# Attention maxima with a fused mask, the planner's durations changed, and more buffers in a hybrid trunk on one core

## The chip, the cores and the metric

One core of a Trainium2 chip runs the whole kernel: TensorE (PE) with its weight loads (PEld), VectorE (DVE), ScalarE (ACT), GpSimd (POOL), and 16 DMA engines whose transfers are all issued from SyncE's queue (SP). The metric is device time in microseconds. The kernel before took 2701.05 us, the median of 3 runs (2700.61 to 2704.6).

## The reference

One layer (D = 1024, 2048 rows, fp32): `h = RMSNorm(x)`, one wide projection of `h`, three branches, a gated merge, an output projection, a residual and a last RMSNorm. The change lies in the first branch, attention with a forget gate over 8 heads of 64, and in the merge.

```python
def block(args):                       # 128 queries against all keys
    s = jnp.einsum('bqhd,bkhd->bhqk', q_blk, k) * scale
    s = s + F_blk[..., :, None] - F[:, :, None, :]      # F: running sum of log-sigmoid
    s = jnp.where(pos[None, None, None, :] <= p_blk[None, None, :, None], s, -jnp.inf)
    p = jax.nn.softmax(s, axis=-1)
    return jnp.einsum('bhqk,bkhd->bqhd', p.astype(v.dtype), v)
...
proj = jnp.einsum('bsnc,ncd->bsnd', ys, w_branch)       # three branches
gate = jax.nn.sigmoid(gates + b_merge).reshape(B, S, N_BRANCH, D)
merged = jnp.sum(gate * proj, axis=2)
return x + merged @ w_out
```

The maximum that softmax subtracts cancels, so any number near it does, if all terms of a query use the same one.

## The kernel before

**Two streams of work.** PE is fed from two sources. A generator `dense()` goes through the wide projection (tiles `pd_in`), then the merge (tiles `pbr`, `pba`) and the output projection (`pout`). Every dense product is three fp32r matmuls, high times high, high times low, low times high. Beside it the parts of `part_side()` run one after the other: norm, logits, memory attention, the delta-rule branch (`part_gdn_a`, `part_gdn_inv`, `part_gdn_b`), then the attention (`part_fox`). A dense matmul is the filler wherever a part has to wait.

**What sets the order.** `Plan` counts planned time while the program is written out: `pl.act(n)`, `pl.dve(n)` and `pl.pool(n)` add a duration for n elements a partition to an engine and return when the result is there. A part yields a time from which it can go on; `run` takes the first part in its list that is ready at PE's planned time, and the dense generator if none is. So the planner's durations decide how many dense matmuls stand between a part's steps on PE. Dependencies and semaphores come from the tile framework, which may move an instruction ahead of others. The engines wait in hardware wherever the plan was too optimistic.

**The attention** (`part_fox`) works in 32 units n = (head h, group G of 512 queries, G = 0 to 3), each with three steps. `maxima()`: for every block of 512 keys and 128 queries, one matmul into `psm`, a mask on the diagonal block (L1108, an addition of `mneg`), a maximum along the keys (L1110) into `nmx`; then the maximum over blocks (L1116), split into a rounded high part and a rest (L1118, L1119) in columns 96 to 103 of `mt`, transposed by PE (`ptm`) and spread into rows 96 to 103 of `QA` (L1124), from which the next product subtracts it. `values()`: for every 128 keys, two matmuls into `pst` (L1227, L1228), two exponentials on ACT (L1234 rounded into `ph`, L1236), the rounding rest on DVE (`plo`, L1191), the running sum of `ph` on POOL (`acc`, L1214), two matmuls onto the values (L1253, L1254). `sums()`: the row sums through PE (`pL`), a trip through DRAM to `lr`, their total and its reciprocal (L1162, L1163), and the product with `oT` on POOL. PSUM has four banks that `psm` (at most two of them) and `pst` (at most three) share.

**The merge** runs as tiles of 128 by 512: `branch(n, g, ...)` goes over d = 0 to 7 for branch n and group g, in the order n = 1, 2, 0. A tile is 12 matmuls; DVE multiplies by the gate tile `gt` (L1463), POOL adds the earlier partial sum `pp` (n = 2 and 0 only, L1467), and the result is stored to `dpt`. `gt`, `pp` and the store are 256 KB each. All loads and stores stand in SP's one queue in program order, and a store waits there for POOL. Branch 0 of groups 0 and 1 needs the attention's results; groups 2 and 3 of it come last, as `pba`, when the attention's buffers are gone.

## Time and profile before

| | us |
|---|---|
| median of 3 runs | 2701.05 |
| the profiled execution | 2707.26 |
| its span, first to last instruction | 2705.4 |
| PE busy | 2593.4 |
| PE idle | 112.0 |
| DVE busy | 1434.6 |
| ACT busy | 1086.6 |
| POOL busy | 941.3 |

A row of the page is read so: "busy" is the time in which at least one instruction of the engine ran; "idle before" is the engine's idle time just ahead of a group, with the engine and line that ended it. [...] The attention runs from about 1511 us to about 2425 us.

### The profile page before, as it was taken

The page shows a single profiled execution, that of the slowest core. Times are in us where ns is not written, and L with a number is a line of the kernel's source. Part 1 is how long each engine was busy: PE and PEld are TensorE (multiplying, and loading weights), DVE is VectorE, ACT ScalarE, POOL GpSimd, SP SyncE. Part 2 cuts the span into 40 slices and gives each one's busy share as a digit, 9 for nine tenths or more (in the row PEclk, how much of TensorE's full clock was granted, in tenths as well). Part 3 has the DMA queues.
Part 4 walks back from the last instruction along what each step waited for, and adds up shares of the span by engine and source line. Part 5 has one row for each costly group of instructions (what it writes and reads, how often), then busy time and mean ns, then how long its engine had stood idle before and what let it go on. Part 6 is the DMA issues. An engine that isn't in the chain of part 4 may idle for free. (4 is left out here: it accounts for less than half of the span.)

```text
span 2705.4 us, 36503 instructions
## 1 busy us (share of the span) xinstructions
PE 2593.4 (96%) x12584; PEld 2119.3 (78%) x12584; DVE 1434.6 (53%) x2867; ACT 1086.6 (40%) x2269; POOL 941.3 (35%) x752
## 2 busy tenths in 40 slices
PE   7999999999999989999999999999999999988998
PEld 6778888888888867888878877877776777757887
DVE  6452556666435583122220287666767778764543
ACT  5442324442665311234332255545655445451221
POOL 0101110011344311122212266756766477783200
PEclk9999999999999999999999999999998999999999
DMA  5223231222667533455542343323326777638433
GB/s 197 70 80 117 75 98 63 71 78 76 204 234 238 195 123 131 120 166 150 160 147 90 117 128 118 102 93 108 96 71 202 229 211 223 207 99 254 169 125 109
DMA packets 264905, 375.00 MB, mean 139 GB/s; under 512 B 62464, under 2 KB 140416, under 8 KB 264464
## 3 DMA queue, kind: packets, MB, share of 16 engines
q1 hardware_dynamic: 264720, 372.68, 43.1%
q8 instruction: 99, 1.62, 0.3%
q14 instruction: 86, 0.70, 0.1%
HBM read 230.66 MB, written 141.92 MB: 138 GB/s over the span
## 5 line engine op out<-in xcount | busy, mean ns | idle before, releaser
L395 PE MATMUL pd_in<-hh,wh_in 128*128 128x512 f32 x1984 | 800.4, 403 | 19.3 <-DVE evl L425 14.4
L397 PE MATMUL pd_in<-hh,wl_in 128*128 128x512 f32 x1984 | 779.1, 393 | 1.0
L396 PE MATMUL pd_in<-hl,wh_in 128*128 128x512 f32 x1984 | 777.7, 392 | 0.0
L379 POOL TENSOR_TENSOR wl_in<-wr_in,wh_in 128x1024 fp32r<-128x1024 f32 x88 | 213.8, 2429 | 967.4 <-ACT wh_in L375 950.9
L395 PEld LDWEIGHTS pd_in<-hh,wh_in 128*128 128x128 f32 x1984 | 374.2, 189 | 102.1 <-DVE evl L425 19.4
L397 PEld LDWEIGHTS pd_in<-hh,wl_in 128*128 128x128 f32 x1984 | 373.9, 188 | 84.4 <-POOL wl_in L379 4.5
L396 PEld LDWEIGHTS pd_in<-hl,wh_in 128*128 128x128 f32 x1984 | 374.7, 189 | 68.9
L1214 POOL TENSOR_TENSOR acc<-acc,ph 128x512 f32<-128x512 f32 (+3 forms) x288 | 323.3, 1123 | 69.8 <-ACT ph L1234 50.4
L1234 ACT ACTIVATE ph<-pst 128x512 fp32r<-128x512 f32 (+1 forms) x320 | 170.6, 533 | 155.8 <-PE pst L1228 64.9
L1191 DVE TENSOR_TENSOR plo<-pst,ph 128x512 fp32r<-128x512 f32 (+1 forms) x320 | 192.0, 605 | 69.0 <-ACT pst L1236 66.8
L1110 DVE TENSOR_REDUCE nmx<-psm 128x1 f32<-128x512 f32 (+2 forms) x320 | 190.0, 605 | 39.9 <-PE psm L1105 37.1
L1236 ACT ACTIVATE pst<-pst 128x512 f32<-128x512 f32 (+1 forms) x320 | 170.9, 534 | 0.0
L375 ACT CAST wh_in<-wr_in 128x1024 fp32r<-128x1024 f32 x88 | 92.4, 1049 | 160.6 <-PE pd_in L396 142.1
L1438 PE MATMUL pbr<-yh,wbh 128*128 128x512 f32 x320 | 131.2, 412 | 7.0 <-DVE gt L1463 6.0
L1439 PE MATMUL pbr<-yl,wbh 128*128 128x512 f32 x320 | 129.3, 405 | 0.7 <-DVE yl L604 0.7
L1440 PE MATMUL pbr<-yh,wbl 128*128 128x512 f32 x320 | 128.9, 403 | 0.0
L1254 PE MATMUL pq<-plo,Vs 128*128 128x512 f32 (+1 forms) x320 | 118.7, 374 | 8.9 <-DVE plo L1191 8.9
L1227 PE MATMUL pst<-QA,KA 128*128 128x512 f32 (+1 forms) x320 | 118.2, 370 | 5.0 <-DVE nmx L1110 1.8
L1467 POOL TENSOR_TENSOR gt<-gt,pp 128x512 f32<-128x512 f32 x64 | 85.6, 1342 | 104.2 <-DVE gt L1463 93.5
L1253 PE MATMUL po<-ph,Vs 128*128 128x512 f32 (+1 forms) x320 | 119.4, 376 | 1.4 <-ACT ph L1234 1.2
L1105 PE MATMUL psm<-KA,QA 68*128 68x512 f32 (+2 forms) x320 | 114.8, 374 | 5.6 <-DVE nmx L1110 5.6
L466 DVE SCALAR_TENSOR_TENSOR evv<-xb,cw,evv 128x512 f32<-128x512 f32 x144 | 116.6, 809 | 3.7
(334 smaller groups left out, 4366.5 us busy)
## 6 DMA issues: line engine op xcount, KB each, us to landing
wr_in<-in_w_in SPq DMA_DIRECT2D x88, 512.0 KB
dgt<-evg SPq DMA_DIRECT2D x96, 256.0 KB
gt<-dgt SPq DMA_DIRECT2D x96, 256.0 KB
dpt<-gt SPq DMA_DIRECT2D x80, 256.0 KB
pp<-dpt SPq DMA_DIRECT2D x64, 256.0 KB
dgq<-evv SPq DMA_DIRECT2D x48, 256.0 KB
kqv<-dgq SPq DMA_DIRECT2D x16, 768.0 KB
xt<-in_x SPq DMA_DIRECT2D x16, 512.0 KB
```

Of the source, the lines that this page charges most:

```text
L379: nc.gpsimd.tensor_sub(lo, raw, hi.bitcast(F32))
L395: nc.tensor.matmul(ps, wh[:, k, :], xh[:, k, :], start=(k == 0), stop=False)
L396: nc.tensor.matmul(ps, wh[:, k, :], xl[:, k, :], start=False, stop=False)
L397: nc.tensor.matmul(ps, wl[:, k, :], xh[:, k, :], start=False, stop=(k == kt - 1))
L1110: nc.vector.tensor_reduce(nmx[:, j, ck:ck + 1], ps[:, 0:w], AX.X, ALU.max)
L1191: nc.vector.tensor_sub(plo[:, 0:w], ps[:, 0:w], ph[:, 0:w].bitcast(F32))
L1214: nc.gpsimd.tensor_add(acc[:, c0:512], acc[:, c0:512], ph[:, 0:w].bitcast(F32))
L1234: nc.scalar.activation(ph[:, 0:w], ps[:, 0:w], AF.Exp, scale=0.125)
L1236: nc.scalar.activation(ps[:, 0:w], ps[:, 0:w], AF.Exp, scale=0.125)
L1438: nc.tensor.matmul(ps, wh[:, k, :], yh, start=(k == 0), stop=False)
L1439: nc.tensor.matmul(ps, wh[:, k, :], yl, start=False, stop=False)
L1440: nc.tensor.matmul(ps, wl[:, k, :], yh, start=False, stop=(k == 3))
```

## The change

- **Mask and maximum.** The diagonal block's mask addition and the maximum become one `tensor_tensor_reduce` (add, then maximum); `mneg` grows to 512 columns. In the built program this is two instructions, the main one and one that writes the maximum out.
- **One rounded maximum a query.** The maximum over blocks is written straight into `mt` as one fp32r number, columns 96 to 99; the copy and the subtraction go, and rows 100 to 103 of `KA`, `QA` and `blk` with them.
- **Sums.** The total of the two halves in `lr` is a `tensor_reduce` over one input instead of an addition of two.
- **Planner.** Other durations for ACT, DVE, POOL, for the delta rule's inverse and for the step to `mt`. `sums` parts are put first in the list of parts.
- **Buffers.** `NQ` 3 to 4 (query tiles), three `psm` banks instead of two, `acc` 2 to 3, `OB` 3 to 4 (output tiles); `values()` may start when the sums of unit n - 3 are done, not n - 2.
- **Gate tiles.** In `branch` the gate tile is loaded two tiles ahead, the partial sum one tile ahead as before.

```diff
     def act(self, n, after=0.0):
-        return self.op("act", 0.2 + 0.00083 * n, after)
+        return self.op("act", 0.17 + 0.00085 * n, after)
     def dve(self, n, after=0.0):
-        return self.op("dve", 0.08 + 0.00104 * n, after)
+        return self.op("dve", 0.15 + 0.00105 * n, after)
     def pool(self, n, after=0.0):
-        return self.op("pool", 0.1 + 0.0022 * n, after)
+        return self.op("pool", 0.19 + 0.0022 * n, after)
...
-    def add(self, gen):
+    def add(self, gen, first=False):
...
-        self.parts.append(part)
+        self.parts.insert(0 if first else len(self.parts), part)
...
-                    t1 = pl.op("dve", 0.18 + 0.0021 * i * i, t1)
+                    t1 = pl.op("dve", 0.35 + 0.0027 * i * i, t1)
...
-        rs, rp = banks.user(2), banks.user(3)
+        rs, rp = banks.user(3), banks.user(3)
...
-        NK, NQ = 6, 3
+        NK, NQ = 6, 4
...
+                        mx = nmx[:, j, ck:ck + 1]
                         if ck == G:
-                            nc.vector.tensor_tensor(ps[:, w - P:w], ps[:, w - P:w], mneg, ALU.add)
-                            e = pl.dve(P, e)
-                        nc.vector.tensor_reduce(nmx[:, j, ck:ck + 1], ps[:, 0:w], AX.X, ALU.max)
+                            nc.vector.tensor_tensor_reduce(ps[:, 0:w], ps[:, 0:w], mneg[:, 512 - w:512], 1.0, -3e38,
+                                                           ALU.add, ALU.max, mx)
+                        else:
+                            nc.vector.tensor_reduce(mx, ps[:, 0:w], AX.X, ALU.max)
...
-                mx = nmx[:, :, 0]
-                if G:
-                    mx = fx.tile([P, 4], F32, tag="mx", name="mx", bufs=2)
-                    nc.vector.tensor_reduce(mx, nmx[:, :, 0:G + 1], AX.X, ALU.max)
-                mv = mt[:, 96:104].rearrange("p (j s) -> p j s", s=2)
-                nc.vector.tensor_copy(mv[:, :, 0], mx)
-                nc.vector.tensor_sub(mv[:, :, 1], mx, mv[:, :, 0].bitcast(F32))
-                t1 = pl.op("dve", 0.5, e)
+                nc.vector.tensor_reduce(mt[:, 96:100], nmx[:, :, 0:G + 1], AX.X, ALU.max)
+                t1 = pl.op("dve", 0.25, e)
...
-            nc.vector.tensor_tensor(rl, lr[:, 0], lr[:, 1], ALU.add)
+            nc.vector.tensor_reduce(rl, lr.rearrange("p s j -> p j s"), AX.X, ALU.add)
...
-                yield (lambda: mready.get(n, INF) if min(st["L"], st["gate"]) >= n - 1 else INF), 0.0
-                acc = fx.tile([P, 512], F32, tag="acc", name="acc", bufs=2)
+                yield (lambda: mready.get(n, INF) if st["L"] >= n - 2 and st["gate"] >= n - 1 else INF), 0.0
+                acc = fx.tile([P, 512], F32, tag="acc", name="acc", bufs=3)
...
-                pl.add(sums(n, oS, acc, fill["ta"]))
-
-        OB = 3
+                pl.add(sums(n, oS, acc, fill["ta"]), True)
+
+        OB = 4
...
-                if d < 7:
-                    load_gate(n, g, d + 1, True)
-                elif then:
-                    load_gate(*then, 0, True)
+                for e in (d + 1, d + 2):
+                    if e < 8:
+                        load_gate(n, g, e, e - d)
+                    elif then:
+                        load_gate(*then, e - 8, e - d)
...
-                pp = None
-                if n != 1:
-                    pp = bp.tile([P, 512], F32, tag="pp", name="pp", bufs=3)
-                    move(pp, dpt[n // 2][g][:, d, :], 256)
-                gates[n, g, d] = gt, pp
+                gates[n, g, d] = [gt, None]
+            ld = gates[n, g, d]
+            if n != 1 and ahead < 2 and ld[1] is None:
+                ld[1] = bp.tile([P, 512], F32, tag="pp", name="pp", bufs=3)
+                move(ld[1], dpt[n // 2][g][:, d, :], 256)
```

The planner's numbers move instructions on all engines. Three places follow, before and after, as the built programs have them.

DVE at the end of the last unit's maxima, before: the last diagonal block, then the step from `nmx` to `mt`.

```order
L1108 TENSOR_TENSOR psm<-psm,mneg 128x128
L1110 TENSOR_REDUCE nmx<-psm 128x1
L1116 TENSOR_REDUCE mx<-nmx 128x4
L1191 TENSOR_TENSOR plo<-pst,ph 128x512
L1118 CAST mt_12279<-mx 128x4
L1119 TENSOR_TENSOR mt_12279<-mx,mt_12279 128x4
```

The same place after (ISA is the fused instruction and its write-out; L1462 is the gate product, L1078 and L1121 are L1077 and L1124 of before).

```order
L1110 ISA psm,nmx<-psm,mneg 128x512
L1110 ISA nmx 128x1
L1116 TENSOR_REDUCE mt_12283<-nmx 128x4
L1078 TENSOR_TENSOR Vs_12230<-ptv,Vs_12230 128x4x64
L1462 SCALAR_TENSOR_TENSOR gt<-gt,pbr_1_20800 128x512
L1121 TENSOR_TENSOR QA_12223<-ptm,blk 4x512
```

From the last block's maximum to the transposed `mt` there is one instruction of DVE where there were three, with a fourth of another step among them.

PE near the end of the last unit's values, before:

```order
L1227 MATMUL pst<-QA_12221,KA_12209 128x512
L1228 MATMUL pst<-QB_12224,KB_12215 128x512
L1253 MATMUL po<-ph,Vs_12227 128x512
L1254 MATMUL pq<-plo,Vs_12227 128x512
L1227 MATMUL pst<-QA_12221,KA_12209 128x384
L1228 MATMUL pst<-QB_12224,KB_12215 128x384
```

The same key tiles after (L1224, L1225, L1250, L1251 are L1227, L1228, L1253, L1254 of before; L1436 to L1438 are a branch tile's matmuls, and `pbr_1` is branch 2, group 1, since the listing drops the branch's digit).

```order
L1224 MATMUL pst<-QA_12223,KA_12209 128x512
L1225 MATMUL pst<-QB_12227,KB_12215 128x512
L1250 MATMUL po<-ph,Vs_12229 128x512
L1251 MATMUL pq<-plo,Vs_12229 128x512
L1436 MATMUL pbr_1_21071<-yh,wbh_20419 128x512
L1437 MATMUL pbr_1_21071<-yl,wbh_20419 128x512
L1438 MATMUL pbr_1_21071<-yh,wbl_20421 128x512
L1224 MATMUL pst<-QA_12223,KA_12209 128x384
L1225 MATMUL pst<-QB_12227,KB_12215 128x384
```

Before, the last unit's steps follow each other with nothing between them; after, matmuls of branch 2 stand between them. Behind the last `pL` of the attention there are 10.5 branch tiles before and 26.75 after, all ahead of the first `pba`.

SP's queue where branch 2 ends and branch 0 begins, before (`dpt_3` is the store of branch 2, group 3; `dgt_115` and `dpt_0` are the gate and the partial sum for branch 0, group 0; `wbr` a weight tile of branch 0):

```order
L243 DMA dpt_3_134<-gt 128x512
L243 DMA wbr<-in_w_br 128x512 x2
L243 DMA lr<-dL_227 128x2x4
L243 DMA dya_121<-oT 64x512
L243 DMA za<-dza_101 64x512
L243 DMA gt<-dgt_115 128x512
L243 DMA pp<-dpt_0_131 128x512
```

The same place after:

```order
L243 DMA dpt_3_134<-gt 128x512
L243 DMA pp<-dpt_3_138 128x512
L243 DMA wbr<-in_w_br 128x512
L243 DMA gt<-dgt_115 128x512
L243 DMA dpt_3_134<-gt 128x512
L243 DMA pp<-dpt_0_131 128x512
```

The attention's small transfers are gone from here, and the next branch's gate tile is asked for before branch 2's stores are all out.

## Rows read from the trace of the kernel before

**Rows 1.** The page's first part: busy time of an engine over the whole span, its share, instructions.
```profile
PE 2593.4 (96%) x12584; PEld 2119.3 (78%) x12584; DVE 1434.6 (53%) x2867; ACT 1086.6 (40%) x2269; POOL 941.3 (35%) x752
```

**Rows 2.** The busy time of each engine in nine stretches: the stretch (us), its length, then PE, PEld, DVE, ACT and POOL busy with their instructions, the granted clock of TensorE as a share of 2.4 GHz, the mean busy share of the 16 DMA engines, GB/s.
```profile
0.00:430.00 430.00, 400.49 (x1935) 329.13 (x1936) 221.61 (x385) 162.07 (x261) 50.77 (x29) 0.98 0.32 103
430.00:900.00 470.00, 464.49 (x2248) 381.83 (x2247) 250.97 (x563) 228.31 (x603) 123.64 (x105) 1.00 0.45 147
900.00:1100.00 200.00, 185.55 (x825) 149.66 (x824) 109.58 (x175) 36.10 (x71) 36.48 (x25) 0.99 0.39 134
1100.00:1511.00 411.00, 406.60 (x2375) 342.17 (x2374) 83.77 (x190) 144.42 (x303) 87.68 (x52) 1.00 0.45 140
1511.00:1800.00 289.00, 287.43 (x1328) 231.72 (x1327) 187.19 (x404) 140.78 (x273) 171.10 (x148) 1.00 0.38 117
1800.00:2350.00 550.00, 524.97 (x2349) 421.21 (x2348) 401.29 (x792) 268.28 (x540) 361.02 (x306) 0.98 0.53 162
2350.00:2427.00 77.00, 65.13 (x256) 45.32 (x255) 57.64 (x111) 46.56 (x95) 67.82 (x58) 0.96 0.35 107
2427.00:2473.00 46.00, 36.77 (x157) 29.23 (x155) 13.56 (x20) 4.09 (x7) 18.38 (x15) 0.92 0.81 249
2473.00:2705.00 232.00, 221.95 (x1125) 189.03 (x1125) 109.02 (x229) 56.01 (x118) 24.42 (x17) 0.98 0.45 151
```

**Rows 3.** What PE waited for between 1800 and 2350 us: total us, times, longest.
```profile
PE ptm L1123 <- DVE mt L1119: 8.1, 6, 2.8
PE psm L1105 <- DVE nmx L1110: 5.1, 6, 2.8
PE ptv L1075 <- DVE nmx L1110: 3.9, 2, 2.7
PE pq L1254 <- DVE plo L1191: 3.2, 1, 3.2
```

**Rows 4.** The timeline of DVE, of POOL and of PE near 1838 us: start, duration, engine, line, operation; in brackets the idle time before it and what ended it.
```profile
1835.31 3.65 DVE L1118 CAST mt<-nmx 128x4 fp32r<-128x4 f32 x1
1838.88 0.15 DVE L1162 TENSOR_TENSOR rl<-lr 128x4 f32<-128x4 f32 x1
...
1836.61 2.33 POOL L379 TENSOR_TENSOR wl_in<-wr_in,wh_in 128x1024 fp32r<-128x1024 f32 x1
...
1839.22 0.32 PE L1123 MATMUL ptm<-ident,mt 128*104 128x128 f32 x1 [2.83 <-DVE mt L1119]
```

**Rows 5.** DVE's groups by shape between 1511 and 2427 us: line, operation, out<-in, count | busy us, mean ns of one | idle before.
```profile
L1191 DVE TENSOR_TENSOR plo<-pst,ph 128x512 fp32r<-128x512 f32 x224 | 152.9, 685 | 56.0 <-ACT pst L1236 54.3
L1110 DVE TENSOR_REDUCE nmx<-psm 128x1 f32<-128x512 f32 x224 | 151.3, 686 | 38.6 <-PE psm L1105 37.1
...
L1108 DVE TENSOR_TENSOR psm<-psm,mneg 128x128 f32<-128x128 f32 x128 | 36.1, 293 | 26.8 <-PE psm L1105 25.6
...
L1162 DVE TENSOR_TENSOR rl<-lr 128x4 f32<-128x4 f32 x31 | 21.7, 701 | 14.7 <-DMA lr<-dL 14.7
...
L1118 DVE CAST mt<-mx 128x4 fp32r<-128x4 f32 x24 | 13.9, 577 | 0.5
...
L1119 DVE TENSOR_TENSOR mt<-mx,mt 128x4 fp32r<-128x4 f32 x24 | 10.3, 429 | 0.5
...
L1118 DVE CAST mt<-nmx 128x4 fp32r<-128x4 f32 x8 | 8.9, 1112 | 0.0
...
L1119 DVE TENSOR_TENSOR mt<-nmx,mt 128x4 fp32r<-128x4 f32 x8 | 4.5, 558 | 0.1
...
L1116 DVE TENSOR_REDUCE mx<-nmx 128x4 f32<-128x16 f32 x8 | 1.3, 167 | 0.2
```

**Rows 6.** The one DVE line that also writes out a running sum: min/median/max ns of the main instruction and of the reading of the accumulator.
```profile
L329 DVE SCALAR_TENSOR_TENSOR jkv<-xt x2: 1204/1638/2073, 5.8 to 12.1; 128x1024 f32<-128x1024 f32 x2
L329 DVE DVE_READ_ACCUMULATOR jkv<-xt x2: 77/79/81, 6.9 to 14.1; 128x1 f32 x2
```

**Rows 7.** Two more groups by shape, of POOL (all of the span) and of ACT (1500 to 2410 us), columns as in the group of DVE.
```profile
L1214 POOL TENSOR_TENSOR acc<-acc,ph 128x512 f32<-128x512 f32 x192 | 250.7, 1306 | 44.1 <-ACT ph L1234 34.7
...
L1234 ACT ACTIVATE ph<-pst 128x512 fp32r<-128x512 f32 x223 | 133.1, 597 | 93.2 <-PE pst L1228 64.9 <-DVE pst L1231 9.7 <-issue 7.2
```

**Rows 8.** PE's timeline: its longest wait behind 1511 us.
```profile
2398.47 0.79 PE L1254 MATMUL pq<-plo,Vs 128*128 128x512 f32 x1 [4.88 <-DVE plo L1191]
```

**Rows 9.** The branch tiles behind the attention: the first matmul, the last eviction and the first matmul of the next stage in the timelines of PE and DVE, and what PE waited for between 2427 and 2480 us.
```profile
2427.57 0.39 PE L1438 MATMUL pbr<-yh,wbh 128*128 128x512 f32 x1
...
2466.42 0.69 DVE L1463 SCALAR_TENSOR_TENSOR gt<-gt,pbr 128x512 f32<-128x512 f32 x1 [2.89 <-PE pbr L1440]
...
2473.13 1.01 PE L1563 MATMUL pba<-yh,wbh 128*128 128x256 f32 x3 [3.57 <-ACT yh L603]
...
PE pbr L1438 <- DVE gt L1463: 5.8, 3, 3.3
```

**Rows 10.** What the DMA queue of SP waited for between 2427 and 2473 us.
```profile
SPq L243 <- POOL gt L1467: 18.0, 9, 3.9
```

**Rows 11.** One stretch in which PE does almost nothing but 512-column matmuls, columns as in the nine stretches.
```profile
600.00:700.00 100.00, 100.00 (x449) 82.96 (x448) 59.31 (x96) 32.49 (x63) 12.66 (x6) 1.00 0.31 92
```

**Rows 12.** What PE waited for between 900 and 1100 us.
```profile
PE pd_in L395 <- DVE evl L425: 14.4, 10, 4.5
```

More of the change, by code (lines that the diff above doesn't have):

```diff
@@ L1021, in part_fox @@
         ones = fx.tile([P, P], F32R, name="ones")
-        mneg = fx.tile([P, P], F32, name="mneg")
+        mneg = fx.tile([P, 512], F32, name="mneg")
         nc.gpsimd.memset(mneg, 0.0)
-        nc.gpsimd.affine_select(mneg, mneg, [[-1, P]], ALU.is_ge, -1e30, base=0, channel_multiplier=1)
+        nc.gpsimd.affine_select(mneg[:, 384:512], mneg[:, 384:512], [[-1, P]], ALU.is_ge, -1e30, base=0,
+                                channel_multiplier=1)
         mnegT = fx.tile([P, P], F32, name="mnegT")
@@ L1033, in part_fox @@
             nc.vector.memset(KA[i][64:68].bitcast(F32), 1.0)
-            nc.vector.memset(KA[i][96:104].bitcast(F32), -1.0)
+            nc.vector.memset(KA[i][96:100].bitcast(F32), -1.0)
             nc.gpsimd.memset(Vs[i][:, :, P:192].bitcast(F32), 2.0)
@@ L1038, in part_fox @@
         nc.gpsimd.memset(blk, 1.0)
-        nc.gpsimd.affine_select(blk, blk, [[-2, 4], [0, P]], ALU.is_ge, 0.0, base=-96, channel_multiplier=1)
-        nc.gpsimd.affine_select(blk, blk, [[2, 4], [0, P]], ALU.is_ge, 0.0, base=97, channel_multiplier=-1)
-        mts = [fx.tile([P, 104], F32R, name=f"mt{i}") for i in range(2)]
+        nc.gpsimd.affine_select(blk, blk, [[-1, 4], [0, P]], ALU.is_ge, 0.0, base=-96, channel_multiplier=1)
+        nc.gpsimd.affine_select(blk, blk, [[1, 4], [0, P]], ALU.is_ge, 0.0, base=96, channel_multiplier=-1)
+        mts = [fx.tile([P, 100], F32R, name=f"mt{i}") for i in range(2)]
         for i in range(2):
@@ L1447, in dense, with load_gate @@
         gates = {}
-        def load_gate(n, g, d, ahead=False):
+        def load_gate(n, g, d, ahead=0):
             if (n, g, d) not in gates:
```

6 lines of the change are left out of this document (3 added, 3 removed).

## The prediction

> **What bounds the kernel now.** I read the busy times first: PE is busy 2593.4 of 2705.4 us, so 112.0 us of idle time are all that a better order can win, and the time that TensorE spends at its lower clock [rows 1]. No matmul is added or taken away, so PE's work stays. Next the stretches [rows 2], to see where those microseconds lie. [...] From 0 to 1511 us PE idles 53.9 us. In the attention's first stretch, 1511 to 1800, it idles 1.6 us at a clock of 1.00. From 1800 to 2350 it idles 25.0 us and loses 0.02 x 550 = 11.0 us to the clock. From 2350 to 2427: 11.9 and 3.1 us. From 2427 to 2473: 9.2 and 3.7 us. From 2473 on: 10.1 and 4.6 us. So the attention and the branch tiles behind it, which the change moves, lose 37.6 us up to 2350 and 27.9 us after it, 65.5 us together.
>
> Then who is waited for. Between 1800 and 2350 the four longest waits, 20.3 of 25.0 us, all end with DVE [rows 3], which is busy only 73% of that stretch. So it is late now and then, not always. One such place in full: a copy of 128x4 numbers into `mt` (L1118) takes 3.65 us, and it ends at 1838.96 where POOL's 2.33 us subtraction (L379) ends, at 1838.94; PE has stood 2.83 us for `mt` by then [rows 4]. The groups say that this is common: L1118, L1119 and L1162 take 429 to 1112 ns in the mean for four numbers a partition, while the reduction L1116, of one input with as many results, takes 167 ns [rows 5]. While such an instruction stands, everything behind it on DVE (`plo`, `nmx`, the gate product) stands too.
>
> **The change, part by part.** *Mask and maximum.* 128 mask additions of 293 ns go, 36.1 us [rows 5]. The fused instruction has no row. From below: as long as the maximum alone, since L1110 and the two-input L1191 take 686 and 685 ns for 512 columns. From above: L329, which also writes out a sum, took 1204 ns once and 2073 the other time, a factor of 1.72, so up to 0.49 us more each, 63 us in all [rows 6]. Its reading of the accumulator takes 79 ns [rows 6], 10 us for 128. I take the lower end, because the second operand is in SBUF and the first in PSUM, as in L1191: 26 us of DVE saved. *One maximum.* L1118 and L1119 go, 13.9 + 8.9 + 10.3 + 4.5 = 37.6 us [rows 5]; eight more reductions of 0.17 us come, so 36 us saved, and the way from the last maximum to PE's transpose loses two instructions. *Sums.* L1162's 21.7 us become 31 reductions of 0.17 us: 16 us saved. Together 78 of DVE's 646 us between 1511 and 2427 [rows 2]. None of it is PE's, so it counts only through PE's waits.
>
> *Planner and buffers.* The old numbers give 0.61 us for 512 columns on DVE, 1.23 on POOL, 0.63 on ACT; the rows say 0.69, 1.31 and 0.60 [rows 5, 7]; the new ones give 0.69, 1.32 and 0.61. So the old order let PE come to a DVE or POOL result too early. In the new order the heads repeat almost instruction for instruction, and matmuls of branch 2 stand between the last unit's steps, where there were none: PE's 4.88 us wait at 2393 lies there [rows 8]. More query, sum and output tiles and a third `psm` bank can only let a step start earlier; the larger `mneg` costs POOL a fraction of a microsecond once. Of the 37.6 us, the best case is the rate of the quiet first stretch, 1.6 us in 289, over 840 us: 5 us stay. The worst is that all stays. I take 10, close to the low end, since both the blocked instructions and the too short durations go: 27.6 us won.
>
> *Branch tiles.* This part gives back. The attention ends earlier in PE's order, so 26.75 branch tiles instead of 10.5 run behind its last `pL`, with nothing to fill in. A tile is 12 matmuls; at 449 in 100 us [rows 11] that is 2.67 us. Before, 10.5 tiles took from 2427.57 to 2466.42, so 3.70 us each [rows 9]. Each moves 256 KB of gate, 256 of partial sum, 256 of store and on average 128 of `y`, 917,504 bytes; at 3.70 us that is 248 GB/s, and the stretch shows 249 at a DMA share of 0.81 [rows 2]. With all DMA engines busy it would be 249 / 0.81 = 307 GB/s, and a tile 2.99 us. Eight tiles (branch 2, group 3) also load 256 KB of the next weights, 0.85 us at that rate. From below: 26.75 x 0.32 + 8 x 0.85 = 15 us lost. From above, at the old pace: 26.75 x 1.03 + 8 x 0.85 = 34 us. PE waited there for the gate product [rows 9]; a gate tile two ahead takes away its wait for `gt`, but SP's queue, which stood 18.0 of 46 us for POOL in front of a store [rows 10], stays in order. Behind a load that waits for a free gate buffer now stand the stores and the attention's small transfers. I take 24 us, the middle. The wait of 3.57 us for the attention's last `y` before `pba` [rows 9] goes, as does the thin end of the attention: 27.9 - 24 = 3.9 us won.
>
> *The rest, at nothing.* PE's 14.4 us for evictions behind the delta rule's inverse [rows 12] stay: DVE's order of steps and evictions there is the same in both programs; the planner's larger number for a step may still put more matmuls between them on PE, so up to 5 us may be won. Matmuls of the memory attention and the delta rule change places by a few; PE idles 10 us in those stretches (430 to 900, 1100 to 1511), so up to 5 us either way.
>
> **Sum.** 27.6 + 3.9 = 31.5 us. The profiled execution has a span of 2705.4 us and took 2707.26; it becomes 2673.9 and 2675.8. It lay 6.2 us above the median of the runs, 2701.05, so the forecast for that is 2670.
>
> **The rivals.** *Everything is covered.* The attention keeps 5 us of loss and the branch tiles run with all DMA engines busy, 15 us: 65.5 - 20 = 45 us won, 2656. For it speaks that `gt` no longer comes in the tile in which it is used; against it that no stretch in the rows shows a share over 0.81. [...]
>
> *The tiles keep their old pace,* 34 us: 65.5 - 10 - 34 = 21 us won, 2680. The queue on SP speaks for it.
>
> *DVE is not relieved.* The fused instruction runs 1.72 times as long, which takes back 63 of the 78 us, or PE's waits were never the planner's: the attention keeps its 37.6 us, the tiles cost 24, and 4 us are won, 2697. Against it speaks that the wait at 1838 us hangs on an instruction that goes [rows 4]. [...]
>
> *Slower: SP's queue chokes the branch tiles.* 26.75 tiles without filler, each with a load that waits for one of five gate buffers, a store that waits for POOL, and, in eight, a weight tile. From 4.95 us a tile on, (65.5 - 10 + 5.4) / 26.75 = 2.28 us over PE's 2.67, the kernel is slower; at 5.3 us it loses 70 us there and comes to 2716. Against it: 4.95 us means 185 GB/s, and 10.5 tiles have run at 248.
>
> **How the numbers follow.** Chances: the forecast 0.50, everything covered 0.15, old pace 0.17, DVE not relieved 0.09, slower 0.09. A run of this kernel can tell about 0.2%, 5.4 us, from no change. The first three are faster, 0.82 and 0.01 of the fourth; the rest of the fourth, 0.08, is within 0.2%; 0.09 is slower. The range goes from 2646, the covered case with 5 us won from the moved matmuls and 5 from the evictions, to 2695, short of the unrelieved case: outside lie the slower case, most of the fourth and a few hundredths below.
>
> **What would show it.** In the changed kernel's groups: the fused instruction near 0.69 us at 512 columns with 0.08 behind it, the reductions into `mt` and `rl` near 0.17 us, and DVE some 78 us less busy. In PE's waits: those for `mt` gone, those for `nmx` and `plo` below 10 us in all up to the last `pL`. In the stretches: a tile pace between 3.0 and 3.7 us behind the attention, with a DMA share over 0.81, and the wait before `pba` gone. The forecast is wrong if that pace is over 3.7 us, if DVE's small reductions still take as long as POOL's instructions, or if the first 1511 us lose more than now.

## The result: 0.54% faster, about half of what was forecast

The changed kernel took 2690.15 us (median of 5 runs, 2682.22 to 2691.65), the kernel before 2704.6 us on the same chip (5 runs, 2700.61 to 2706.46): a ratio of 0.9946, 95% interval 0.9928 to 0.9963, so 14.5 us less. The forecast was 31.5 us less; the time lies in its range. The profiled execution took 2691.65 us and has a span of 2689.9 us, against 2705.4 before: 15.5 us less, and this difference is what is split up below.

The page's first part of the kernel after; it answers to [rows 1].

```profile
PE 2581.4 (96%) x12584; PEld 2124.4 (79%) x12584; DVE 1373.2 (51%) x2813; ACT 1093.2 (41%) x2273; POOL 939.2 (35%) x752
```

DVE is busy 61.4 us less (forecast 78), and PE 12.0 us less with the same 12584 matmuls. Where the time went is not in this line. Three milestones at which PE has the same work behind it in both orders tell more: the first `psm` (the attention begins), the first `pba` (all 80 branch tiles are done) and the end. The view of one tile gives first and last start; its row for `psm` in the kernel before, then after:

```profile
L1105 PE MATMUL psm<-KA,QA x320: 221/395/648, 1549.0 to 2374.4; 68*128 68x512 f32 x98, 68*128 68x384 f32 x31, 68*128 68x128 f32 x29, 68*128 68x256 f32 x2
```

```profile
L1106 PE MATMUL psm<-KA,QA x320: 222/395/628, 1560.7 to 2311.4; 68*128 68x512 f32 x96, 68*128 68x128 f32 x32, 68*128 68x384 f32 x32
```

So the attention begins **11.7 us later** than before. The same view of `pba` gives a first start at 2466.2 before and 2453.3 after. From `psm` to `pba` it took 917.2 and 892.6 us, **24.6 us won**; from `pba` to the end 239.2 and 236.6, 2.6 won. 24.6 + 2.6 - 11.7 = 15.5. The attention and the branch tiles nearly gave what was forecast for them; the part that was entered at nothing took much of it back.

These two stretches, cut at the milestones, columns as in [rows 2], of the kernel before:

```profile
0.00:1549.00 1549.00, 1495.12 (x7544) 1234.25 (x7545) 674.66 (x1330) 578.57 (x1247) 309.79 (x226) 0.99 0.40 130
...
1549.00:2466.20 917.20, 872.95 (x3891) 692.88 (x3890) 650.26 (x1307) 451.49 (x904) 605.83 (x508) 0.98 0.48 149
```

and of the kernel after:

```profile
0.00:1560.70 1560.70, 1501.19 (x7544) 1239.81 (x7545) 687.94 (x1331) 584.61 (x1251) 309.73 (x226) 0.99 0.40 129
...
1560.70:2453.30 892.60, 857.01 (x3890) 692.72 (x3889) 579.55 (x1255) 453.97 (x906) 604.37 (x509) 0.98 0.50 154
```

The matmuls are the same to one. Ahead of the attention PE's idle time grew by 5.6 us (53.9 to 59.5) and its **busy** time by 6.1; in the attention and the tiles its idle time fell by 8.7 (44.3 to 35.6) and its busy time by 15.9. So busy time holds more than work, and idle time alone tells a third of this gain. One part of it can be seen in a timeline: near 2298 us three 512-column matmuls on end start at 2298.49, 2298.72 and 2298.96 and are shown as 0.40 us each, so one that starts 0.16 us late leaves no gap. What the 15.9 us consist of is not shown. DVE's busy time fell by 70.7 us between the two milestones and grew by 13.3 ahead of the first.

Where it lies, in finer stretches of the kernel after:

```profile
900.00:1100.00 200.00, 188.53 (x804) 153.45 (x804) 109.12 (x177) 37.73 (x81) 35.90 (x26) 0.97 0.40 137
1100.00:1511.00 411.00, 401.36 (x2359) 337.08 (x2359) 96.82 (x192) 149.13 (x307) 87.65 (x53) 0.99 0.45 138
...
1561.00:2093.00 532.00, 529.88 (x2479) 430.07 (x2477) 369.70 (x858) 322.07 (x643) 391.80 (x330) 1.00 0.37 111
2093.00:2364.00 271.00, 250.90 (x1089) 201.00 (x1090) 180.52 (x356) 117.84 (x242) 167.07 (x144) 0.95 0.65 197
2364.00:2453.00 89.00, 75.62 (x322) 61.11 (x321) 29.03 (x41) 13.96 (x22) 45.19 (x36) 0.94 0.84 280
```

Four things are to be seen. From 900 to 1100 us PE idles 3.0 us less than in [rows 2] (11.5 against 14.5), but the granted clock is 0.97 instead of 0.99, which loses 0.02 x 200 = 4 us more. (The traces record this clock as a share, 1.00 or 0.50: in the kernel before 1.00 from 2440 to 2443 us, where 512-column matmuls start 0.23 us apart, and 0.50 from 2463 to 2465, where they start 0.43 us apart. So the loss is one minus the mean share, times the stretch. No run shows a frequency, so the 2.4 GHz in the legend of [rows 2] stands for a share of 1.00 and no more.) From 1100 to 1511 us PE is busy 5.2 us less, and DVE, with nearly the same instructions (192 against 190), is busy 13 us **more** (96.82 against 83.77). From 1561 to 2093 us, the attention beside the wide projection, PE is idle 2.1 us in 532. And from 2093 to 2364 us, where branch tiles lie beside the attention, 20.1 us of idle time and 0.05 x 271 = 13.6 us of clock are still lost. Behind the last `pL`, 26.75 tiles took 2453.3 - 2364.0 = 89.3 us, 3.34 us a tile (forecast 3.0 to 3.7). One of PE's waits there, from 2364 to 2480 us, is long; it is for the first `y` of branch 0:

```profile
PE pbr L1436 <- ACT yh L603: 9.0, 1, 9.0
```

DVE's groups by shape from 1511 to 2430 us, after; they answer to [rows 5].

```profile
L1113 DVE TENSOR_REDUCE nmx<-psm 128x1 f32<-128x512 f32 x192 | 128.7, 684 | 24.6 <-PE psm L1106 22.6
...
L1110 DVE CUSTOM_DVE_ANT_0 psm<-psm,mneg 128x512 f32<-128x512 f32 x32 | 22.8, 711 | 0.0
...
L1110 DVE CUSTOM_DVE_ANT_0 psm<-psm,mneg 128x384 f32<-128x384 f32 x32 | 18.2, 569 | 12.5 <-PE psm L1106 12.5
L1110 DVE DVE_READ_ACCUMULATOR2_ANT nmx<- 128x1 f32 x128 | 17.9, 140 | 0.0
...
L1110 DVE CUSTOM_DVE_ANT_0 psm<-psm,mneg 128x256 f32<-128x256 f32 x32 | 14.1, 440 | 2.3 <-PE psm L1106 2.1
...
L1110 DVE CUSTOM_DVE_ANT_0 psm<-psm,mneg 128x128 f32<-128x128 f32 x32 | 9.2, 287 | 0.1
...
L1159 DVE TENSOR_REDUCE rl<-lr 128x4 f32<-128x8 f32 x32 | 5.0, 155 | 14.7 <-DMA lr<-dL 14.6
...
L1116 DVE TENSOR_REDUCE mt<-nmx 128x4 fp32r<-128x16 f32 x8 | 1.3, 166 | 0.2
```

Mask and maxima together: 128.7 + 22.8 + 18.2 + 17.9 + 14.1 + 9.2 = 210.9 us, against 151.3 + 17.6 + 13.3 + 9.1 + 36.1 = 227.4 before: 16.5 saved where 26 were forecast, 7.8 of the difference because the maximum's write-out takes 140 ns and not the 79 ns of [rows 6]. The sums fell from 21.7 to 5.0 us, and the step to `mt` is one instruction of 0.17 us, as forecast. PE's wait for `mt` from 1800 to 2350 us, 8.1 us in [rows 3], became:

```profile
PE ptm L1120 <- DVE mt L1116: 0.9, 2, 0.6
```

### The profile page after: what moved, and what is told of

It reads as the page before. It is cut to its first block, busy times and chain, and to the rows that moved or that the text cites. A ratio compares the mean times of both kernels' runs of the same rounds, so it can differ in the third digit from the quotient of the medians.

```text
span 2689.9 us, 36468 instructions
## 1 busy us (share of the span) xinstructions
PE 2581.4 (96%) x12584; PEld 2124.4 (79%) x12584; DVE 1373.2 (51%) x2813; ACT 1093.2 (41%) x2273; POOL 939.2 (35%) x752
## 4 chain that ended last, share of the span: by engine, by line
PE 74%; DVE 7%; DMA 6%; issue 5%; POOL 4%; ACT 4%; SPq 1%; POOLq 0%; DVEq 0%; ACTq 0%
PE pd_in L395 14%; PE pd_in L397 13%; PE pd_in L396 13%; PE psm L1106 2%; PE pout L1594 2%; PE pout L1593 2%; PE pout L1592 2%; PE pst L1225 2%; PE po L1250 2%; PE pq L1251 2%; PE pst L1224 2%; DVE tmp L831 2%; PE pbr L1436 1%; PE pbr L1437 1%; PE pbr L1438 1%
## 5 line engine op out<-in xcount | busy, mean ns | idle before, releaser
L395 PE MATMUL pd_in<-hh,wh_in 128*128 128x512 f32 x1984 | 803.0, 405 | 18.4 <-DVE evl L425 11.5
L1436 PE MATMUL pbr<-yh,wbh 128*128 128x512 f32 x320 | 131.9, 413 | 18.1 <-ACT yh L603 10.3
L1113 DVE TENSOR_REDUCE nmx<-psm 128x1 f32<-128x512 f32 x192 | 128.7, 684 | 24.6 <-PE psm L1106 22.6
L1438 PE MATMUL pbr<-yh,wbl 128*128 128x512 f32 x320 | 128.3, 402 | 0.0
L1250 PE MATMUL po<-ph,Vs 128*128 128x512 f32 (+1 forms) x320 | 118.4, 371 | 4.8 <-ACT ph L1231 4.8
L1224 PE MATMUL pst<-QA,KA 128*128 128x512 f32 (+1 forms) x320 | 116.0, 362 | 3.1 <-DVE QA L1121 3.1
L1251 PE MATMUL pq<-plo,Vs 128*128 128x512 f32 (+1 forms) x320 | 117.6, 370 | 0.2 <-DVE plo L1188 0.2
```

What stands on the lines that cost most here:

```text
L395: nc.tensor.matmul(ps, wh[:, k, :], xh[:, k, :], start=(k == 0), stop=False)
L1224: nc.tensor.matmul(ps[:, 0:w], KA[kt][:, ks], QAn[:, c0:512], start=True, stop=False)
L1250: nc.tensor.matmul(po[:, c0:512], V[:, 0:128], ph[:, 0:w], start=(t0 == 0), stop=(t0 == NT - 1))
L1251: nc.tensor.matmul(pq[:, c0:512], V[:, 64:192], plo[:, 0:w], start=(t0 == 0), stop=(t0 == NT - 1))
```

## The experiments

**The theory** after the result: in the attention, PE waited for DVE instructions that stand behind POOL, and these are gone (theory A in most expectations); the planner's new durations brought an order of the delta rule (1089 to 1511 us) that costs PE 10 to 12 us; and the branch tiles keep what is still lost. **The rivals**: the later start is a mishap of one execution; the attention's gain is the durations' work, not the instructions'; or the loss behind 2093 us hangs on one place (the tiles without filler, SP's queue, late `y`). The table has all runs with their milestones: ratio to the kernel before on the same chip with its 95% interval, the first `psm`, then from there to the first `pba`, and from there to the end of the span, in us of the profiled execution.

| run | ratio | first psm | to pba | to end |
|---|---|---|---|---|
| kernel before | 1 | 1549.0 | 917.2 | 239.2 |
| changed kernel | 0.9946 (0.9928 to 0.9963) | 1560.7 | 892.6 | 236.6 |
| changed_again | 0.9938 (0.9925 to 0.9950) | 1561.7 | 894.8 | 233.9 |
| before_new_durations | 1.0050 (1.0037 to 1.0063) | 1558.5 | 917.1 | 241.3 |
| before_dve_instructions | 0.9929 (0.9917 to 0.9942) | 1552.7 | 903.2 | 235.2 |
| one_maximum_alone | 0.9956 (0.9943 to 0.9969) | 1551.7 | 904.8 | 239.9 |
| fused_mask_alone | 0.9963 (0.9950 to 0.9976) | 1550.5 | 910.2 | 237.9 |
| after_old_durations | 0.9911 (0.9897 to 0.9924) | 1550.1 | 896.5 | 234.8 |
| old_until_attention | 0.9902 (0.9889 to 0.9915) | 1550.9 | 891.7 | 235.9 |
| inverse_duration_old | 0.9903 (0.9888 to 0.9919) | 1555.3 | 896.5 | 235.7 |
| inverse_duration_new_alone | 0.9880 (0.9865 to 0.9894) | 1550.0 | 895.7 | 234.9 |
| old_in_delta_rule_alone | 0.9908 (0.9891 to 0.9925) | 1551.7 | 893.7 | 234.4 |
| gates_one_ahead | 0.9886 (0.9873 to 0.9899) | 1551.2 | 892.0 | 234.0 |
| old_buffers_sums_last | 0.9952 (0.9940 to 0.9964) | 1548.9 | 899.3 | 242.6 |
| early_y_branch0 | 0.9890 (0.9874 to 0.9905) | 1550.6 | – | – |
| y_landing_later | 0.9951 (0.9938 to 0.9964) | 1550.7 | 907.0 | 238.1 |
| early_y_and_later_landing | 0.9933 (0.9917 to 0.9948) | 1552.0 | 901.2 | 236.3 |
| stores_on_pool_queue | 1.0002 (0.9993 to 1.0011) | 1551.8 | 921.8 | 232.3 |
| latency_050_in_attention | 0.9902 (0.9886 to 0.9919) | 1550.9 | 886.6 | 239.2 |
| latency_043_in_attention | 0.9900 (0.9883 to 0.9917) | 1553.0 | 886.3 | 235.0 |

(In `early_y_branch0` the first `pba` runs ahead of the last branch tile, so its milestone doesn't compare.) The milestones of a row are those of one execution, and that lay up to 5 us off the median of its run (2689.17 against 2684.37 in `inverse_duration_old`, 2692.83 against 2688.25 in `before_dve_instructions`). So a few us between two rows' milestones tell nothing by themselves.

### The durations

`old_until_attention`:

```diff
+        self.new = False
-        return self.op("dve", 0.15 + 0.00105 * n, after)
+        return self.op("dve", (0.15 + 0.00105 * n) if self.new else (0.08 + 0.00104 * n), after)
...
-                    t1 = pl.op("dve", 0.35 + 0.0027 * i * i, t1)
+                    t1 = pl.op("dve", 0.18 + 0.0021 * i * i, t1)
...
+        pl.new = True
         yield from part_fox()
```

(`act` and `pool` alike.) 

> The changed kernel, but the planner keeps its old durations (and the old one of the inverse) until the attention's part begins; from there the new ones hold. Theory A (the new durations reorder the delta rule, and that order costs the 11.7 us by which the changed kernel reaches its first psm matmul later): the first psm falls to about 1549 us, the time to about 2679. Rival B (those 11.7 us are start-up and clock of that one execution): the first psm stays near 1560 and the time near 2690.

`before_new_durations`, the kernel before with the four new lines alone. 

> The kernel before with the planner's new durations alone: no instruction, buffer or list order changed. Theory A (the new durations lose 12 us ahead of the attention, and the attention's gain needs the DVE instructions as well as the durations): first psm near 1560 us, first psm to first pba shortened by 5 to 15 of the 24.6 us that the whole change won there, time 2700 to 2712. Rival C (the durations alone make the attention's gain): first psm to first pba shortened by 20 us or more, time near 2692. Rival D (the durations do nothing for the attention): 2714 or more.

`after_old_durations`, the changed kernel with the four old ones. 

> The changed kernel with all of the planner's old durations; instructions, buffers, list order and gate tiles stay as changed. Theory A: no loss ahead of the attention (first psm near 1549 us) and half of the attention's gain, time 2685 to 2693. Rival C (the gain is the durations'): 2702 to 2706. Rival D (the durations give nothing, only cost): 2676 to 2680.

Measured: with old durations up to the attention it begins at 1550.9 us and the kernel gains another 12 us (0.9902 against 0.9946). The durations alone make the kernel before 0.5% **slower**, 2721.04 us: 9.5 us ahead of the attention and 917.1 against 917.2 in it. So the theory's 5 to 15 us there were wrong, and rival D, that they do nothing for the attention, was right. In the changed kernel they give the attention 896.5 - 891.7 = 4.8 us in the profiled executions; the whole time of the two runs differs within their intervals. With the old ones it took 2683.14 us, faster than the theory's 2685 to 2693 and slower than rival D's 2676 to 2680.

`changed_again` is the changed kernel once more. 

> The changed kernel itself, once more, on the chip of the three runs beside it. If the cost ahead of the attention belongs to the order that all new durations together make (first psm at 1560.7 us; 1558.5 in the kernel before with the new durations; 1550.9 with old ones up to the attention), the first psm comes at 1557 to 1562 us again and the ratio is 0.993 to 0.996. If it was a mishap of that execution, 1549 to 1552 us and 0.989 to 0.991.

 It came to 1561.7 us and 0.9938: no mishap.

`inverse_duration_old` takes back the inverse's number alone, `inverse_duration_new_alone` adds it to `old_until_attention`, and `old_in_delta_rule_alone` sets `pl.new` to False ahead of `part_gdn_inv` and to True again ahead of `part_fox`. 

> The changed kernel with one duration old, that of a step of the delta rule's inverse (0.18 + 0.0021 i i us); all other new ones hold from the start. The changed kernel gave a ratio of 0.9946 to the kernel before, with old durations up to the attention 0.9902, so 0.0044 or 12 us lie in the durations ahead of the attention. Theory A (the inverse's longer steps push the delta rule's second part 20 us later, and its chains then wait): the ratio is 0.990 to 0.992 and the first psm at 1550 to 1554 us. Rival B (the general durations of DVE, ACT and POOL make the worse order): 0.993 to 0.995, first psm at 1557 to 1561.

> The counterpart: old durations up to the attention, but the new one for a step of the inverse; new ones from the attention on. Theory A: ratio 0.993 to 0.995, first psm at 1557 to 1561 us. Rival B: 0.990 to 0.992, first psm at 1550 to 1554. If both runs lie between, each part costs some, or the loss needs both.

> The new durations of ACT, DVE and POOL hold everywhere but in the inverse and the delta rule's second part, which keep the old ones, the inverse's own too. Theory A (the delta rule's order costs the time): first psm at 1549 to 1553 us, ratio 0.988 to 0.991. Rival L (the cost comes from the parts before it): the first psm at 1554 to 1561 us, ratio 0.991 to 0.995.

Measured: 1555.3, 1550.0 and 1551.7 us, and ratios of 0.9903, 0.9880 and 0.9908. So the parts ahead of the inverse cost nothing to speak of with the new durations (1551.7): it is the order of the inverse and the delta rule's second part. The inverse's number costs nothing by itself. The general ones without it cost nothing by the ratio (0.9903 against 0.9902 with both old); the profiled execution, the slowest of five, begins the attention 4.4 us later. The whole loss of some 12 us needs both. Theory A had the place right, but neither it nor rival B, which each blamed one number, came out in both runs.

Much of what is slower there shows in one instruction. Line L291 is a step of the reciprocal root that scales the delta rule's output `ob`, which PE transposes next (`pR`). It has the row, before and then after (ns min/median/max):

```profile
L291 DVE TENSOR_SCALAR gbt<-gbt x16: 169/170/1268, 1110.2 to 1433.7; 128x4 f32<-128x4 f32 x16
```

```profile
L291 DVE TENSOR_SCALAR gbt<-gbt x16: 169/1268/1294, 1131.7 to 1468.5; 128x4 f32<-128x4 f32 x16
```

The timeline of DVE, POOL and PE at one such place, after:

```profile
1152.85 0.16 DVE L290 TENSOR_TENSOR gbt<-gbt,so 128x4 f32<-128x4 f32 x1
1153.01 1.28 POOL L867 TENSOR_TENSOR U<-U,m 128x512 f32<-128x512 f32 x1 [16.34 <-PE pB L873]
1153.05 1.27 DVE L291 TENSOR_SCALAR gbt<-gbt 128x4 f32<-128x4 f32 x1
1154.35 0.16 DVE L292 TENSOR_TENSOR ro<-gbr,gbt 128x4 f32<-128x4 f32 x1
1154.55 0.69 DVE L981 TENSOR_TENSOR ob<-pO,ro 128x512 f32<-128x512 f32 x1
1155.39 0.30 PE L988 MATMUL pR<-ident,ob 128*128 128x128 f32 x1 [0.46 <-DVE ob L981]
```

and before, where POOL's masking (L867) starts 1.35 us after the step that scales `ob`:

```profile
1130.17 0.17 DVE L291 TENSOR_SCALAR gbt<-gbt 128x4 f32<-128x4 f32 x1
1130.38 0.16 DVE L292 TENSOR_TENSOR ro<-gbr,gbt 128x4 f32<-128x4 f32 x1
1130.57 0.69 DVE L981 TENSOR_TENSOR ob<-pO,ro 128x512 f32<-128x512 f32 x1
1131.92 1.28 POOL L867 TENSOR_TENSOR U<-U,m 128x512 f32<-128x512 f32 x1 [18.73 <-PE pB L873]
```

After, POOL's L867 starts at 1153.01, DVE's four numbers a partition take 1.27 us and end with it, at 1154.32 and 1154.29. That is the stall of [rows 4], back in another part: the new order lets POOL begin inside the chain. In 10 of the 16 places after, L291 starts 0.02 to 0.04 us behind L867 and takes 1.27 to 1.29 us; at 1131.74, where it starts 0.01 us ahead of L867, it takes 0.17. Why it lasts as long as POOL's instruction, no run shows. PE waits for `ob` from 1100 to 1560 us, before and then after:

```profile
PE pR L988 <- DVE ob L981: 4.3, 3, 2.7
```

```profile
PE pR L988 <- DVE ob L981: 9.4, 10, 2.7
```

L291's mean by run: 289 ns before, 959 after, 960 in `before_new_durations` and `changed_again`, 839 in `inverse_duration_old`, and 288 or 289 in `old_until_attention`, `after_old_durations`, `inverse_duration_new_alone` and `old_in_delta_rule_alone`. PE's busy time from 1100 to 1511 us goes with it: 401.3 to 401.4 us in the three runs with 959 or 960, 405.4 in `inverse_duration_old`, 406.6 in these four and in the kernel before.

So the growth of PE's idle time in that stretch, 5.2 us, is this wait, which grew by 5.1. Not shown is that the stall is all of the 10 to 12 us: `inverse_duration_old` has most of it, yet PE waits only 5.6 us for `ob` there and the ratio shows no loss, and no run took away the stall and kept the order. The clock of 0.97 from 900 to 1100 us is not the rest: `inverse_duration_new_alone` and `old_in_delta_rule_alone` have 0.97 there too and lose nothing.

### The instructions and the buffers

`before_dve_instructions` is the kernel before with `mneg` of 512 columns, the fused instruction, one rounded maximum and the sums as a reduction, as in the change's diff. `one_maximum_alone` keeps of this

```diff
-                nc.vector.tensor_copy(mv[:, :, 0], mx)
-                nc.vector.tensor_sub(mv[:, :, 1], mx, mv[:, :, 0].bitcast(F32))
+                nc.vector.tensor_reduce(mt[:, 96:100], nmx[:, :, 0:G + 1], AX.X, ALU.max)
```

with the four rows that go, and `fused_mask_alone` the `tensor_tensor_reduce`. The plan goes with the instructions: the step to `mt` counts 0.25 instead of 0.5 us in the first two runs, and the mask's addition is no longer counted in the first and the third. So instructions and order are not told apart. The sums' reduction was not run alone.

> The kernel before with the DVE instructions of the change alone: fused mask and maximum, one rounded maximum, sums as a reduction; durations, buffers, list order and gate tiles as before. Theory A (the blocked small DVE instructions make a good part of PE's waits): PE's waits for mt between 1800 and 2350 us, 8.1 us before, fall below 2, the first psm to first pba stretch shortens by 8 to 15 us, time 2690 to 2697. Rival C (the waits are the order's): less than 4 us won, 2701 to 2706. Rival D (these instructions make the whole gain): 24 us or more, 2680 or less.

> The kernel before with one rounded maximum a query as its one change: the reduction writes straight into mt, the copy and the subtraction go; mask and maximum stay two instructions, the sums an addition of two. The three instruction changes together gave 0.9929. Theory A (two small DVE instructions that stand behind POOL's work were what PE waited for): half of that or more, ratio 0.994 to 0.9965, PE's waits for mt between 1800 and 2350 us below 2 us. Rival G (the mask's 26 us of DVE time carry the gain): 0.997 to 1.000.

> The kernel before with the fused mask and maximum as its one change. Theory A: a smaller part, ratio 0.996 to 0.999, the waits for mt stay at 5 us or more. Rival G: 0.993 to 0.996.

Measured: 0.9929, 0.9956 and 0.9963. Both single ratios lie where theory A had them; rival G is out by the first, while the second lies 0.0003 from its range, less than its interval. By the medians the parts won 10.9 and 7.9 us, which add up to the 18.8 of all three. PE's waits from 1800 to 2350 us, with all three instructions:

```profile
PE psm L1106 <- DVE nmx L1113: 7.7, 7, 2.0
PE pq L1251 <- DVE plo L1188: 3.8, 7, 0.9
...
PE ptm L1120 <- DVE mt L1116: 0.2, 1, 0.2
```

with one maximum alone:

```profile
PE ptv L1076 <- DVE nmx L1112: 5.1, 3, 2.3
PE ptm L1119 <- DVE mt L1115: 4.6, 3, 1.8
```

and with the fused mask alone:

```profile
PE ptm L1124 <- DVE mt L1120: 11.8, 5, 5.6
```

The wait for `mt`, 8.1 us in [rows 3], is gone with both (0.2) and stays, larger, with the mask alone. With the maximum alone it is 4.6, not below 2 as expected, perhaps since the mask's instructions still stand ahead of the last block; that was not tried.

`old_buffers_sums_last` and `gates_one_ahead` start from `old_until_attention` and take back `NQ`, the `psm` banks, `acc`, `OB`, the start of `values` and the list order, or `load_gate` and its loop. 

> Old durations up to the attention, new ones from there (ratio 0.9902), and the attention's buffers and list order as before: three query tiles, two psm banks, two acc, three output tiles, values one unit behind the sums, sums last in the list. Theory A (DVE's instructions alone won 18.9 us, ratio 0.9929, and the buffers with the gate tile the next 7): 3 to 7 us slower, ratio 0.991 to 0.993, the last pL at 2365 to 2400 instead of 2353 us. Rival F (buffers and list order give nothing): ratio 0.990, the last pL within 5 us of 2353.

> Old durations up to the attention, new ones from there (ratio 0.9902), and the gate tile one tile ahead as in the kernel before. Theory A (the branch tiles wait for SP's queue and the transfers, and the gate tile two ahead takes a part of that away): 3 to 8 us slower than with two ahead, ratio 0.991 to 0.993, and PE's waits for the gate product behind the last pL rise. Rival E (the second gate tile only takes buffers and puts a wait at the head of SP's queue): equal or faster, ratio 0.988 to 0.990.

Measured: without the buffers 0.9952 instead of 0.9902, a loss of 13 us, 7.6 of it ahead of `pba` and 6.7 behind; the last `pL` comes at 2422 us, later than expected. The six edits of this run were not tried one by one, and 13 us is what they are worth beside the new durations in the attention: with the old durations, the instructions alone gave 0.9929 and the instructions, buffers and gate tiles 0.9911 (`after_old_durations`, on the same chip), 5 us. With the gate tile one ahead 0.9886: that part of the change brings nothing (rival E, as far as the intervals tell).

### The branch tiles

One place in the mixed stretch of the kernel after, 2297 to 2307 us, in the timelines of DVE, ACT and PE:

```profile
2296.98 0.28 DVE L1188 TENSOR_TENSOR plo<-pst,ph 128x128 fp32r<-128x128 f32 x1
...
2300.09 0.62 ACT L1139 CAST ah<-acc 128x512 fp32r<-128x512 f32 x1 [4.01 <-POOL acc L1211]
...
2302.43 0.62 ACT L603 CAST yh<-yr 128x512 fp32r<-128x512 f32 x1 [1.71 <-DMA yr<-dym]
2303.08 0.75 DVE L604 TENSOR_TENSOR yl<-yr,yh 128x512 fp32r<-128x512 f32 x1 [5.82 <-ACT yh L603]
...
2306.51 0.47 PE L1106 MATMUL psm<-KA,QA 68*128 68x128 f32 x1 [5.75 <-DVE nmx L1113]
```

DVE stands 5.82 us for the split of `y`. ACT had stood 4.01 us for POOL's `acc`, but what came last was the transfer of `y`, 1.71 us more. The maximum is queued behind the split, and PE waits 5.75 us for that. Five runs, all from `old_until_attention`, tried to take such waits away.

```diff
-                return raw, move(raw, src_y[n][g][:, k, :], 256)
+                return raw, move(raw, src_y[n][g][:, k, :], 256) + 6.0
```

> Old durations up to the attention, new ones from there (ratio 0.9902), and the planner takes a y tile to land 6 us later than it did, so that its split (ACT, then DVE) is written later in these engines' order. Theory J (splits that wait for y at the head of DVE's queue hold up the attention's maxima and products in the mixed stretch): DVE's wait of yl for yh between 2080 and 2353 us, about 20 us, falls below 10, PE's wait for nmx below 3 us, 4 to 12 us won, ratio 0.986 to 0.9887. Rival K (y then only comes too late for PE): the waits move to PE's yh, ratio 0.990 or more.

`early_y_branch0` adds `load_ya` from the third tile of branch 2, group 3; the next run has both edits.

```diff
                 if i + 1 < len(seq):
                     nxt.append(load_y(*seq[i + 1], range(4)))
+                else:
+                    pl.add(load_ya())
...
```

(The definition of `load_ya` moves ahead with it; group 1 still waits for the end of branch 2.) 

> Old durations up to the attention, new ones from there (0.9902), and the loads of y for branch 0, group 0 asked for in the third tile of branch 2, group 3, as those of the other groups are, instead of after its last tile. PE's wait for yh at the start of branch 0 was 9.0 us in the changed kernel. Theory H (that wait is the late request): it falls below 2 us, ratio 0.986 to 0.988. Rival I (the transfers there are bound by the DMA engines, so the wait only moves to the gate tiles or to later y): less than 3 us won, 0.989 to 0.991.

> As the first of these four, and y for branch 0, group 0 asked for in the third tile of branch 2, group 3 (that alone gave 0.989). If theory J holds and the gains add: ratio 0.984 to 0.987. Rival: as the early y alone, 0.988 to 0.990.

`stores_on_pool_queue`:

```diff
-            move(dpt[(n + 1) % 3 // 2 if n else 2][g][:, d, :], gt, 256, w)
+            nc.gpsimd.dma_start(dpt[(n + 1) % 3 // 2 if n else 2][g][:, d, :], gt)
```

(`move` also counts a transfer in the plan, so the stores are no longer counted there either, and other instructions may change places.) 

> Old durations up to the attention, new ones from there (ratio 0.9902), and the branch tiles' stores are issued by POOL, right behind its addition, instead of by SP. Theory M (stores that wait for POOL at the head of SP's queue hold up the gate tiles and y): SP's wait for POOL's gt between 2080 and 2442 us is gone, y and gates land earlier, 4 to 12 us won, ratio 0.986 to 0.9887. Rival N (the transfers themselves are the limit, or POOL pays for the issuing): ratio 0.989 to 0.995.

`latency_050_in_attention` (and `latency_043_in_attention` with 0.43):

```diff
         pl.new = True
+        pl.LAT = 0.5
         yield from part_fox()
```

> Old durations up to the attention, new ones from there (ratio 0.9902), and from there on the planner takes 0.50 us instead of 0.35 for the way of a result from one engine to the next. The attention's steps then lie further apart, and 5.5 branch tiles instead of 26.75 stand behind the last pL. Theory O (a tile without filler costs 3.36 us, with filler 2.67, and PE waits less for DVE in the attention): up to 21.25 x 0.69 = 14.7 us won, ratio 0.985 to 0.988. Rival P (tiles beside the attention cost as much there, since the transfers or DVE hold them up): 0.989 to 0.993.

> The same with 0.43 us: 16.25 tiles behind the last pL. Theory O: up to 10.5 x 0.69 = 7.2 us won, ratio 0.9875 to 0.989. Rival P: 0.990 to 0.992.

Measured: **`y_landing_later` lost, but didn't test theory J.** DVE's wait of `yl` for `yh` between 2080 and 2353 us rose from 20.0 to 27.1 us instead of falling below 10. The waits moved to PE's `yh`, as rival K had it: 0.9951. The attention ran ahead (last `pL` at 2305.0 instead of 2352.8 us), and 40 tiles behind it took (2457.7 - 2305.0) / 40 = 3.82 us each. PE's waits from 2353 to 2480 us there:

```profile
PE pbr L1438 <- ACT yh L604: 15.9, 2, 12.8
PE pbr L1438 <- DVE gt L1464: 7.6, 6, 3.0
```

The nearest to a test is another run: in `latency_043_in_attention` DVE's wait of `yl` fell to 8.6 us and PE's wait for `nmx` from 7.4 to 3.0, both from 2080 to 2353 us, and the ratio stayed at 0.9900 (0.9883 to 0.9917), where theory J wanted 0.986 to 0.9887. So its gain didn't come there; as that run moves other steps too, theory J is not ruled out.

The early `y` took PE's wait at the start of branch 0 from 10.0 to 1.2 us, and the kernel won 3 us at most, within the intervals: rival I, the wait moved. With the late landing too, it gave 0.9933, slower than with the early `y` alone. **Theory M fell.** With the stores on POOL's queue, SP waited from 2080 to 2442 us, and PE from 2353 to 2480 us, for:

```profile
SPq L244 <- DMA dpt<-gt: 116.9, 50, 4.2
SPq L244 <- POOL gt L1468: 32.1, 23, 4.0
```

```profile
PE pbr L1438 <- DVE gt L1464: 26.1, 7, 6.2
```

SP waits 116.9 us for stores to be done, against 43.5 in `old_until_attention`, and still 32.1 for POOL, against 61.7; PE waits 26.1 us for the gate product, against 1.5. With the 80 stores issued there POOL is busy for 682.3 us from 1511 to 2695 us, against 641.8 from 1511 to 2680 us in `old_until_attention`: 40.5 us more. At 1.0002 the run is slower than rival N had it, too. **Theory O fell** too: with 5.5 or 16.25 tiles behind the last `pL` instead of 26.75, the kernel took as long (0.9902, 0.9900; rival P). Their profiled executions show 5 us won up to the first `pba`, the medians nothing. So moving the tiles into the attention, with its steps further apart, won nothing here, and what holds them in the end stays open; more gate buffers than five were not tried.

## Why the prediction was half right

- **The step that failed is "The rest, at nothing".** It let matmuls of the delta rule "change places by a few", with 5 us either way. The rest lost 11.7 us (12.7 in the second run). In its place the runs showed the planner's durations: with the old ones up to the attention the loss is gone (1550.9 us, 0.9902 against 0.9946). The prediction looked at DVE's order there and at PE's idle time, but not at POOL's start against DVE's chain of small steps; [rows 4] had shown what such a meeting costs, and it was used for the attention only. That wait is 5.1 us of PE; the cause of the rest stays open. At the evictions, where up to 5 us were to be won, PE idled 3.0 us less, but the clock took 4 (900 to 1100 us).
- **"Both the blocked instructions and the too short durations go"**, 27.6 us for the attention: the first half is right, the second isn't. In the profiled executions the instructions alone won 14.0 us from `psm` to `pba`, the buffers and list order another 7.6, the durations 0.1 alone and 4.8 with the rest, which the medians of those two runs don't bear out.
- **The size for attention and tiles together**, 27.6 + 3.9 = 31.5, against 24.6 measured. The loss of the attention didn't fall to 10 us: 35.8 by the stretches (0.0 + 2.1 up to 2093 us, 20.1 + 13.6 then), nearly all beside branch tiles. That `psm` to `pba` still shortened so much comes mostly from PE's busy time, 15.9 us less, which the prediction took as fixed ("PE's work stays").
- **The branch tiles' give-back**: forecast 24 us at 3.0 to 3.7 us a tile, measured 89.3 - 26.75 x 2.67 = 17.9 at 3.34. The price held, the mechanism only in part: 9.0 of the 17.9 us are one wait, for the first `y` of branch 0, which the sum didn't have, and that a tile costs more for want of filler isn't shown, since with 5.5 such tiles the time was the same. The wait before `pba` was misread: 2473.13 in [rows 9] is a later `pba`; the first was at 2466.2.
- **DVE's relief**: 70.7 us instead of 78 from `psm` to `pba`; the write-out cost 8 us more. The fused instruction itself came close to its lower bound (711 against 686 ns).
- **The rivals.** "Everything is covered" is out by the 35.8 us that the attention still loses, "DVE is not relieved" by PE's wait for `mt`, which fell from 8.1 to 0.9 us from 1800 to 2350 us, "the tiles keep their old pace" by 3.34 against 3.70 us. "SP's queue chokes the branch tiles" didn't come, though SP stood 34.8 of 89 us for POOL there. The forecast's last sentence, that it is wrong "if the first 1511 us lose more than now", is what happened.

## What to carry to other kernels

A planner's durations that match the records better needn't give a better order; here the kernel with old ones ahead of the attention is the faster one (0.9902, and 0.9880 to 0.9911 for its neighbours, against 0.9938 and 0.9946). When a table of costs changes, look in the new order at every chain of small DVE instructions on PE's path, and at what POOL starts beside it, not only in the part that the change means. And measure progress between milestones with equal work behind them: idle time alone showed 8.7 of 24.6 us here.

## What was not expected of the hardware

- A fused addition and maximum with one PSUM and one SBUF input takes 711, 569, 440 and 287 ns for 512, 384, 256 and 128 columns, the plain maximum 686, 551, 416 and 284: the mask costs 1 to 6%, and the write-out of the result 140 ns more.
- A `tensor_scalar` of 128x4 numbers on DVE (L291) took 1.27 to 1.29 us instead of 0.17 in the 10 places where a POOL instruction of 1.28 or 1.29 us had begun 0.02 to 0.04 us ahead of it. The 64 small reductions that now write `mt` and `rl` took 146 to 170 ns each, though POOL is busy in 392 of the 532 us from 1561 to 2093; the copy before could take 3.65 us.
- A store that POOL issues saves no time here: PE's wait for the gate product rose to 26.1 us from 2353 to 2480 us, SP's wait for stores to end to 116.9, and POOL was busy for 40.5 us more behind 1511 us.
